# Taking the gated recurrence's logarithms in its projections, and loading its first pair of heads into tiles of the mixer that runs beside them

## The chip, the cores and the metric

One core of a Trainium2 chip runs the whole program. The metric is the device time of one execution in microseconds (us). A run's time is a little longer than the span of its profile, which lasts from the first to the last instruction. The engines are PE (matrix multiply; PEld is its weight load), DVE (vector), ACT (activation functions), POOL (GpSimd) and SP, whose queue issues most DMAs. Each engine works through its own instructions in the order in which they are written into the program.

## The reference, cut to what matters

Two transformer blocks over 512 tokens of width 1024. The second block also reads 256 context tokens and has three mixers side by side: a gated recurrence (4 heads, HGRN), a delta-rule recurrence (4 heads, RWKV) and a windowed attention (8 heads). Their outputs are concatenated, projected by `w_out`, and feed a mixture of 32 experts. The change touches the gated recurrence:

```python
def hgrn2_forget(f_pre, lb):
    f = lb + (1.0 - lb) * jax.nn.sigmoid(f_pre)
    log_f = jnp.log(jnp.maximum(f, HGRN_F_FLOOR))
    k = (1.0 - lb) * jax.nn.sigmoid(-f_pre)
    return to_heads(log_f, A_HEADS), to_heads(k, A_HEADS)
...
cum = jnp.cumsum(log_f, axis=3)                    # within a chunk
decay = exp(cum[t] - cum[s]) for s <= t
scores = jnp.einsum('bhntd,bhnsd,bhntsd->bhnts', q, k, decay)
o_intra = scores @ v;  q_in = q * exp(cum);  k_out = k * exp(cum[-1] - cum)
s = s * exp(cum[-1]) + k_out^T v                   # state from chunk to chunk
...
out = rms_norm(o_forward + flip(o_backward), gn_gain) * silu(g)
```

It runs forwards and backwards, over the context first and then over the latent tokens.

## The kernel before, in words

Block 1 runs first, up to about 800 us. Then comes block 2. `block2_in` makes its normalised input (`hchi`, `hclo` for 256 context tokens, `hlhi`, `hllo` for 512 latent ones, each as a high and a low part), and `rwkv_in` makes the inputs of the RWKV mixer by projections.

`rwkv` and `project` are traced one after the other, and the scheduler mixes them. `rwkv` handles six chunks of 128 tokens, each with a `front` (gates, decays, a 32x32 triangular solve that goes through DRAM by way of the tiles `rsc`, `rB`, `sX`) and a `back` (state update). `project` makes all other projections of the block, those of the attention and of the gated recurrence, by `gemm2` (one 128-column weight tile, split in a high and a low part by ACT at L299 and POOL at L300, then three matmuls for each of eight slices) or `tokens_of`. A result goes from PSUM by ACT into a staging tile `gst` (two buffers) and by an SP DMA to DRAM. Its order is: queries and keys of the attention (L1317), their row sums and reciprocal roots, the attention's values (L1300, L1308), the recurrence's values, queries, then for each pair of heads p and direction d the gate `f` and key `k` (two Sigmoids at L1360, scaled at L1361 and L1362, stored as `hfd` and `hkd`), and last the output gates (L1317 with Silu).

`hgrn` then loads all that for two pairs of heads (`hlf` by L1384, `hk` by L1389, `hq`, `hg`) into tiles on the right side of SBUF, where the tiles of `rwkv` were. It takes the logarithm of the gates: maximum (L1399), Ln with scale 8 (L1400), minus log 8 (L1401), and Ln of the latent keys into `hE` (L1406). The generator `pair` first handles the context (copy on POOL L1421, scan L1423, Exp L1432) and then seven levels (a hierarchical scheme that doubles the block length H from 1 to 64), each with Exps (L1470 to L1475), products, matmuls and four POOL additions (L1486 to L1489). The two pairs take turns. In between, pieces of the output projection run for the RWKV half (`out_first`: `mraw`, `wor`, `woh`, L1720), and after step 9 the first attention head. After the levels come the remaining heads, the rest of the output projection, the router, and the experts, whose weights (`er`) are loaded once the attention's tiles are free.

What sets the order: the Tile framework's scheduler places each engine's instructions by priority and by when it thinks inputs and buffers are there; a tile may reuse the bytes of an older one once all readers of that are done. `issue_after(logs.ins)` keeps the first Exps behind the last Ln on ACT.

Of the kernel before, what the change touches and what calls it, by code (L numbers as in the profile page):

```python
# [18 lines left out]
P = 128  # L19
# [139 lines left out]
def consts3():  # L159
    c = Pack()  # L160
    i = np.arange(P)
    c.add("ident", np.eye(P))
# [8 lines left out]
    f = np.arange(TC) % P  # L171
    c.add("hg_suf", np.broadcast_to((f != P - 1).astype(np.float32), (P, TC)))
    c.add("hg_pre", np.broadcast_to((f != 0).astype(np.float32), (P, TC)))
    return c


C2, C3 = consts2(), consts3()


# [60 lines left out]
def prep2(i):  # L240
# [4 lines left out]
    o["c2"], o["c3"] = C2.array(), C3.array()  # L245
# [27 lines left out]
class Kern:  # L273
# [601 lines left out]
    def c(self, name, rows=P):  # L875
        o, n = self.cat[name]
        return self.cst[:rows, o:o + n]
# [94 lines left out]
    def rwkv_in(self):  # L972
        nc, I, rw = self.nc, self.I, self.rw
        mu = self.v("mu")
# [18 lines left out]
        th, ad = (rw.tile([P, 768], F32, name=n) for n in ("rth", "rad"))  # L993
        k, v = (rw.tile([P, 2, 768], F32, name=n) for n in ("rk", "rv"))
# [25 lines left out]
    def rwkv(self):  # L1020
# [14 lines left out]
        kk = rw.tile([P, 2, 768], F32, name="rkk")  # L1035
# [241 lines left out]
    def project(self):  # L1277
# [4 lines left out]
        self.hqd, self.hgd = dram("hqd", 2, P, T), dram("hgd", 2, P, T)  # L1282
        self.hfd, self.hkd, self.hvd = dram("hfd", 2, 2, P, N), dram("hkd", 2, 2, P, N), dram("hvd", N, 256)
# [4 lines left out]
        def st(n):  # L1288
            return self.gs.tile([P, N], F32, tag="gst", name=self.name("gst"), bufs=2)[:, :n]
# [32 lines left out]

        sums = self.gp.tile([96, T], F32, tag="ss", name="nss", bufs=1)
# [16 lines left out]
        tokens(I["w_hi"], lambda i, o: rows(self.hvd, i, o))  # L1340


        l = self.v("lb")
        lb, nb = (self.gs.tile([P, 4], F32, name=n) for n in ("hlb", "hnb"))
        nc.vector.tensor_sub(lb, l, l)
        nc.scalar.activation(lb, lb, AF.Exp)
        nc.vector.reciprocal(nb, lb)
        nc.vector.tensor_mul(lb, lb, nb)
        nc.vector.tensor_sub(lb, lb, lb)
        nc.vector.tensor_scalar(nb, lb, -1.0, 1.0, OP.mult, OP.add)  # L1350
        for p in range(2):
            columns(I["w_hg"][p], self.hqd[p])
        for p in range(2):
            for d in range(2):
                c = 2 * d + p
                ps = self.gemm2(I["w_hg"][2 + c])
                f, k = st(N), st(N)
                for o, sign in ((f, 1.0), (k, -1.0)):
                    for x, t in zip((o[:, :TC], o[:, TC:]), ps):
                        nc.scalar.activation(x, t, AF.Sigmoid, scale=sign)  # L1360
                nc.vector.tensor_scalar(f, f, nb[:, c:c + 1], lb[:, c:c + 1], OP.mult, OP.add)  # L1361
                nc.vector.tensor_scalar(k, k, nb[:, c:c + 1], None, OP.mult)  # L1362
                nc.sync.dma_start(self.hfd[p, d], f)
                nc.sync.dma_start(self.hkd[p, d], k)
        for p in range(2):
            columns(I["w_hg"][8 + p], self.hgd[p], func=AF.Silu)

    def hgrn(self):
# [6 lines left out]
        def psum(n=T):  # L1375
# [3 lines left out]
        pairs = [([], [], hw.tile([P, T], F32, tag="hq", name=self.name("hq"), bufs=2),  # L1379
                  hw.tile([P, T], F32, tag="hg", name=self.name("hg"), bufs=2)) for _ in range(2)]  # L1380
        for p in range(2):
            for d in range(2):
                pairs[p][0].append(hw.tile([P, N], F32, tag="hlf", name=self.name("hlf"), bufs=4))
                nc.sync.dma_start(pairs[p][0][d], self.hfd[p, d])  # L1384
        self.h_loads = ()
        for p, (lf, kx, q, sgt) in enumerate(pairs):
            for d in range(2):
                kx.append(hw.tile([P, N], F32, tag="hk", name=self.name("hk"), bufs=4))
                nc.sync.dma_start(kx[d], self.hkd[p, d])  # L1389
            self.h_loads = self.h_loads[:1] + (nc.sync.dma_start(q, self.hqd[p]),)  # L1390
            if p == 0:
                others = self.out_first()
                next(others)
                vt = hw.tile([P, 6, 256], F32, name="hvt")
                nc.sync.dma_start(vt, self.hvd.rearrange("(i p) d -> p i d", p=P))
            self.h_loads = self.h_loads[:1] + (nc.sync.dma_start(sgt, self.hgd[p]),)
# [14 lines left out]
        def pair(p, lf, kx, q, sgt):  # L1411
# [4 lines left out]
            for d in range(2):  # L1416
# [14 lines left out]
                with self.tc.issue_after(logs.ins):  # L1431
                    nc.scalar.activation(e, e, AF.Exp)  # L1432
# [924 lines left out]
```

## Time and profile before

| | us |
|---|---|
| three runs | 2075.93, 2077.91, 2082.70 |
| median | 2077.91 |
| the profiled execution | 2081.68 |
| its span | 2079.9 |

| engine | busy us | share of the span |
|---|---|---|
| PE | 1839.3 | 88% |
| PEld | 1303.1 | 63% |
| DVE | 967.7 | 47% |
| ACT | 673.5 | 32% |
| POOL | 573.5 | 28% |

The mean clock granted to TensorE is 0.908 of full speed. A share is an average over very different stages; what the change touches lies between about 850 and 1435 us. In a timeline row the bracket gives how long the engine stood idle before the instruction and what ended that. SPq and ACTq rows are DMA issues.

### The profile page before, as it was taken

The numbers are of one execution on the slowest core, as the hardware profiler recorded it, in microseconds if no ns is written. First come the engines' busy times: TensorE is split into PE (matmuls) and PEld (weight loads), VectorE is DVE, ScalarE is ACT, GpSimd is POOL, SyncE is SP. The second block draws the span as 40 slices with busy tenths as digits, with TensorE's granted clock in tenths as the row PEclk, the third lists the DMA queues.
The fourth block names the chain that finished last, engine by engine and source line by source line (L and its number), as shares of the span: only waits on it lengthen the run. The fifth ranks groups of instructions, "written<-read, shape, count | busy, mean of one in ns | idle before, by whom it ended". The sixth has DMA issues, their size and how long they took to land. (4 is left out here: it accounts for less than half of the span.)

```text
span 2079.9 us, 30469 instructions
## 1 busy us (share of the span) xinstructions
PE 1839.3 (88%) x11941; PEld 1303.1 (63%) x11941; DVE 967.7 (47%) x2052; ACT 673.5 (32%) x1241; POOL 573.5 (28%) x405
## 2 busy tenths in 40 slices
PE   5978899898989999899998999558896999999996
PEld 3656566676757777776777877446675555544442
DVE  5443643575673116435755555576676322222110
ACT  6652324643443234442332223534332101000000
POOL 3222412444346555341211111472100110101011
PEclk9897899999989999996978789668998999999999
DMA  3111223355642225222312122733347999999997
GB/s 132 41 51 32 80 62 109 127 186 182 206 149 71 92 94 204 70 74 63 84 35 72 44 69 93 236 107 114 105 171 273 394 411 416 416 412 415 411 413 277
DMA packets 132668, 363.69 MB, mean 175 GB/s; under 512 B 43884, under 2 KB 63532, under 8 KB 107820
## 3 DMA queue, kind: packets, MB, share of 16 engines
q1 hardware_dynamic: 121916, 340.84, 44.3%
q10 hardware_dynamic: 5472, 15.05, 2.4%
q0 software_dynamic: 5136, 5.85, 1.4%
q8 instruction: 95, 1.56, 0.3%
q14 instruction: 49, 0.40, 0.1%
HBM read 333.02 MB, written 26.55 MB: 173 GB/s over the span
## 5 line engine op out<-in xcount | busy, mean ns | idle before, releaser
L300 POOL TENSOR_TENSOR lo<-wraw,hi 128x1024 fp32r<-128x1024 f32 (+1 forms) x127 | 298.5, 2351 | 587.9 <-ACT hi L299 518.4
L314 PE MATMUL g<-h1hi,hi 128*128 128x512 f32 (+1 forms) x584 | 251.8, 431 | 11.7 <-ACT gt L441 7.5
L316 PE MATMUL g<-h1hi,lo 128*128 128x512 f32 (+1 forms) x584 | 249.5, 427 | 6.5 <-POOL lo L300 6.5
L315 PE MATMUL g<-h1lo,hi 128*128 128x512 f32 (+1 forms) x584 | 251.2, 430 | 3.1 <-DVE h1lo L357 1.6
L2153 PE MATMUL gu<-er,xw 128*64 128x256 f32 x2048 | 237.1, 382 | 8.6 <-issue 3.0
L299 ACT ACTIVATE hi<-wraw 128x1024 fp32r<-128x1024 f32 (+1 forms) x127 | 127.5, 1004 | 313.8 <-PE g L315 154.5
L2153 PEld LDWEIGHTS gu<-er,xw 128*64 128x64 f32 x2048 | 145.3, 137 | 94.8 <-issue 19.9
L2182 POOL DMA_INDIRECT out_dram<-ey,sidx x32 | 49.5, 1547 | 403.6 <-DVE ey L2181 389.8
L314 PEld LDWEIGHTS g<-h1hi,hi 128*128 128x128 f32 (+1 forms) x584 | 117.5, 201 | 46.3 <-ACT gt L441 8.4
L316 PEld LDWEIGHTS g<-h1hi,lo 128*128 128x128 f32 (+1 forms) x584 | 116.9, 200 | 43.9 <-POOL lo L300 11.2
L315 PEld LDWEIGHTS g<-h1lo,hi 128*128 128x128 f32 (+1 forms) x584 | 117.1, 200 | 38.5 <-issue 8.8
L2178 PE MATMUL py<-er,es 128*64 128x512 f32 x512 | 120.4, 603 | 1.4 <-SPq L2224 1.0
L314 PE MATMUL g<-hlhi,hi 128*128 128x512 f32 x200 | 85.2, 426 | 5.0 <-ACT hlhi L951 4.6
L2156 ACT ACTIVATE eg<-gu 128x256 f32<-128x256 f32 x32 | 12.1, 383 | 226.5 <-PE gu L2153 226.5
L315 PE MATMUL g<-hllo,hi 128*128 128x512 f32 x200 | 85.4, 427 | 0.0
L316 PE MATMUL g<-hlhi,lo 128*128 128x512 f32 x200 | 85.3, 427 | 0.0
L2081 PE MATMUL tr<-h,S 128*128 128x512 f32 x256 | 75.1, 426 | 11.3 <-DVE xw L2090 6.7
L2181 DVE SCALAR_TENSOR_TENSOR ey<-py,wslot,g2row 128x512 f32<-128x512 f32 x32 | 24.0, 751 | 117.9 <-PE py L2178 117.9
L2178 PEld LDWEIGHTS py<-er,es 128*64 128x64 f32 x512 | 34.4, 137 | 61.4 <-issue 52.7
L2081 PEld LDWEIGHTS tr<-h,S 128*128 128x128 f32 x256 | 46.8, 198 | 37.4 <-issue 18.3
L898 DVE CUSTOM_DVE_ANT_0 aw<-aw,acc 128x1024 f32<-128x1024 f32 x48 | 64.8, 1355 | 7.7 <-DMA aw<-in_w_ada_dram 7.4
L2157 DVE TENSOR_TENSOR eh<-eg,gu 128x256 f32<-128x256 f32 x32 | 13.3, 417 | 116.5 <-ACT eg L2156 116.5
(659 smaller groups left out, 3689.3 us busy)
## 6 DMA issues: line engine op xcount, KB each, us to landing
er<-in_w_e_dram SPq DMA_DIRECT2D x192, 1024.0 KB
aw<-in_w_ada_dram SPq DMA_DIRECT2D x48, 512.0 KB
wraw<-in_w_qkv_dram SPq DMA_DIRECT2D x36, 512.0 KB
wraw<-in_w_g_dram SPq DMA_DIRECT2D x12, 512.0 KB
dxs<-draw SPq DMA_DIRECT2D x96, 64.0 KB
wraw<-in_w_rw_dram SPq DMA_DIRECT2D x9, 512.0 KB
wraw<-in_w_ga_dram SPq DMA_DIRECT2D x8, 512.0 KB
wraw<-in_w_gb_dram SPq DMA_DIRECT2D x8, 512.0 KB
```

Source lines behind the costliest of these rows:

```text
L299: nc.scalar.activation(hi, raw, AF.Copy)
L300: (lo_engine or nc.gpsimd).tensor_sub(lo, raw, hi.bitcast(F32))
L314: nc.tensor.matmul(ps, lh, rh, start=start, stop=False, **kw)
L315: nc.tensor.matmul(ps, lh, rl, start=False, stop=False, **kw)
L316: nc.tensor.matmul(ps, ll, rh, start=False, stop=stop, **kw)
L898: nc.vector.tensor_tensor_reduce(out=w, in0=w, in1=cc, scale=1.0, scalar=0.0, op0=OP.mult, op1=OP.add, accum_out=self.modl[:, m:m + 1])
L2081: nc.tensor.matmul(ps[:n], S[:, i, :n], self.h2[i][a][:, c], start=i + a == 0, stop=i + a == 4)
L2153: nc.tensor.matmul(ps[64 * c:64 * c + 64, a, :], xs(2 * i + k), w[:, k, a, c, :], start=i + k + a == 0, stop=i == 3 and k == 1 and a == 1, ...
L2157: nc.vector.tensor_mul(hid, g, ps[:, 1])
L2178: nc.tensor.matmul(py[64 * c:64 * c + 64], hs[:, k, 64 * i:64 * i + 64], part[:, k, c, :], start=i + k == 0, stop=i + k == 2)
L2181: nc.vector.scalar_tensor_tensor(y, py, w, self.g2, OP.mult, OP.mult)
L2182: nc.gpsimd.indirect_dma_start(out=self.O["out_0"].rearrange("t (h d) -> (t h) d", h=2), out_offset=bass.IndirectOffsetOnAxis(ap=idx, axis ...
```

## The change

The recurrence's gates, keys, queries, values and output gates are projected first, the attention's inputs last. The two logarithms are taken there: the gate's in place in its staging tile, the key's in a third one, stored in a new DRAM tile `hld`. The staging tag has three buffers. In `rwkv_in` the tiles `rth`, `rad`, `rk`, `rkk` move into a pool `rwf` of their own, which ends at the same address as before but lies below the other tiles. `hgrn` gets a pool `h0` on the left side, whose addresses (105856 to 124288) lie within those of `rwf` (106400 to 124832) but for the first 544, which no later tile before them uses; the first pair's gate, key, log key and query are loaded there. The second pair's stay in `hw`, and the output gates are loaded last. The identity and the scan mask move from the third pack of constants to a fourth, `c4`, which is loaded before `rwkv_in`. `issue_after` falls away.

```diff
@@ rwkv_in
+        th, ad = (self.rwf.tile([P, 768], F32, name=n) for n in ("rth", "rad"))
+        k, self.rw_kk = (self.rwf.tile([P, 2, 768], F32, name=n) for n in ("rk", "rkk"))
...
-        th, ad = (rw.tile([P, 768], F32, name=n) for n in ("rth", "rad"))
-        k, v = (rw.tile([P, 2, 768], F32, name=n) for n in ("rk", "rv"))
+        v = rw.tile([P, 2, 768], F32, name="rv")
@@ project
-            return self.gs.tile([P, N], F32, tag="gst", name=self.name("gst"), bufs=2)[:, :n]
+            return self.gs.tile([P, N], F32, tag="gst", name=self.name("gst"), bufs=3)[:, :n]
...
+        for p in range(2):
+            for d in range(2):
+                c = 2 * d + p
+                ps = self.gemm2(I["w_hg"][2 + c])
+                f, k = st(N), st(N)
+                for o, sign in ((f, 1.0), (k, -1.0)):
+                    for x, t in zip((o[:, :TC], o[:, TC:]), ps):
+                        nc.scalar.activation(x, t, AF.Sigmoid, scale=sign)
+                nc.vector.tensor_scalar(f, f, nb[:, c:c + 1], lb[:, c:c + 1], OP.mult, OP.add)
+                nc.vector.tensor_scalar(k, k, nb[:, c:c + 1], None, OP.mult)
+                nc.sync.dma_start(self.hkd[p, d], k)
+
+                nc.vector.tensor_scalar(f, f, 1e-20, None, OP.max)
+                nc.scalar.activation(f, f, AF.Ln, scale=8.0)
+                nc.vector.tensor_scalar(f, f, float(np.log(8.0)), None, OP.subtract)
+                nc.sync.dma_start(self.hfd[p, d], f)
+                l8 = st(T)
+                nc.scalar.activation(l8, k[:, TC:], AF.Ln, scale=8.0, bias=self.eps(1e-36))
+                nc.sync.dma_start(self.hld[p, d], l8)
+        for p in range(2):
+            columns(I["w_hg"][p], self.hqd[p])
+        tokens(I["w_hi"], lambda i, o: rows(self.hvd, i, o))
+        for p in range(2):
+            columns(I["w_hg"][8 + p], self.hgd[p], func=AF.Silu)
...
@@ hgrn
+        pairs, lk = [], []
+        gates = [self.hg.tile([P, T], F32, tag="hg", name=self.name("hg"), bufs=2) for _ in range(2)]
         for p in range(2):
...
+            to = hw if p else self.h0
+            lf, kx, le = ([to.tile([P, n], F32, tag=f"{t}{p}", name=self.name(t), bufs=2) for _ in range(2)]
+                          for t, n in (("hlf", N), ("hk", N), ("hE", T)))
+            pairs.append([lf, kx, (self.hg if p else to).tile([P, T], F32, tag=f"hq{p}", name=self.name("hq"), bufs=1)])
+            lk.append(le)
...
         for p, (lf, kx, q, sgt) in enumerate(pairs):
...
+            for src, dst in ((self.hfd, lf), (self.hkd, kx), (self.hld, lk[p])):
+                for d in range(2):
+                    nc.sync.dma_start(dst[d], src[p, d])
             self.h_loads = self.h_loads[:1] + (nc.sync.dma_start(q, self.hqd[p]),)
...
-        for lf, *_ in pairs:
-            for x in lf:
-                nc.vector.tensor_scalar(x, x, 1e-20, None, OP.max)
-                logs = nc.scalar.activation(x, x, AF.Ln, scale=8.0)
-                nc.vector.tensor_scalar(x, x, float(np.log(8.0)), None, OP.subtract)
-        lk = []
-        for _, kx, *_ in pairs:
-            lk.append([hw.tile([P, T], F32, tag="hE", name=self.name("hE"), bufs=4) for _ in range(2)])
-            for x, k in zip(lk[-1], kx):
-                logs = nc.scalar.activation(x, k[:, TC:], AF.Ln, scale=8.0, bias=self.eps(1e-36))
...
-                with self.tc.issue_after(logs.ins):
-                    nc.scalar.activation(e, e, AF.Exp)
+                nc.scalar.activation(e, e, AF.Exp)
@@ run
+                pool(es, "pc4", side="right")
+                self.c4 = self.pc4.tile([P, C4.n], F32, name="c4")
+                nc.gpsimd.dma_start(self.c4, self.I["c4"])
...
+                pool(right, "rwf", side="right")
...
+                        pool(e5, "hg")
+                        pool(e5, "h0")
```

How the scheduler's order moves, at three places. SP's queue at the solver of the mixer's fifth and sixth chunk (`rsc`, `rB`, `sX` and `AS` are the solver's tiles), before:

```order
L1145 DMA rsc_8128<-sX_8169 256x1x32 x4
L1125 DMA rsc_8538<-AS_8512 32x8x32 x2
L1148 DMA AS_8101<-rsc_8128 32x8x32 x4
L1127 DMA rB_8544<-rsc_8538 128x1x1024
L1318 DMA hqd<-gst_10072 128x512
L1318 DMA hqd<-gst_10106 128x512
L1363 DMA hfd<-gst_10165 128x768
L1364 DMA hkd<-gst_10166 128x768
```

and now, where `hlf`, `hk`, `hE` are the first pair's gate, key and log key:

```order
L1408 DMA hlf_10516<-hfd 128x768
L1408 DMA hlf_10517<-hfd 128x768
L1323 DMA nkc<-gst_10003 128x256
L1408 DMA hk_10518<-hkd 128x768
L1408 DMA hk_10519<-hkd 128x768
L1408 DMA hE_10520<-hld 128x512
L1408 DMA hE_10521<-hld 128x512
L1151 DMA rsc_8136<-sX_8177 256x1x32 x4
L1131 DMA rsc_8546<-AS_8520 32x8x32 x3
L1154 DMA AS_8109<-rsc_8136 32x8x32 x4
L1131 DMA rsc_8546<-AS_8520 32x8x32
L1325 DMA nqk<-gst_10003 128x512
```

The first pair's loads have come up from behind the mixer's end to stand ahead of the last but one solver's stores; the attention's stores stand where the recurrence's were. SP's queue at the mixer's end (`mix<-ry` stores its output), before:

```order
L1364 DMA hkd<-gst_10364 128x768
L1255 DMA mix<-ry 128x512
L1318 DMA hgd<-gst_10404 128x512
L1384 DMA hlf_10476<-hfd 128x768
L1384 DMA hlf_10478<-hfd 128x768
L1318 DMA hgd<-gst_10438 128x512
L1384 DMA hlf_10480<-hfd 128x768
L1384 DMA hlf_10482<-hfd 128x768
L1389 DMA hk_10484<-hkd 128x768
L1389 DMA hk_10486<-hkd 128x768
L1390 DMA hq_10472<-hqd 128x512
L1720 DMA mraw_10491<-mix 128x512
```

and now:

```order
L1261 DMA mix<-ry 128x512 x2
L1307 DMA nvd<-gst_10461 128x2x256
L1728 DMA mraw_10539<-mix 128x512
L1315 DMA nvw<-gst_10464 128x128 x4
L1728 DMA wor_10543<-in_w_o_dram 128x256
L1408 DMA hlf_10523<-hfd 128x768
L1315 DMA nvw<-gst_10470 128x128 x4
L1728 DMA mraw_10549<-mix 128x512
L1728 DMA wor_10553<-in_w_o_dram 128x256
L1408 DMA hlf_10524<-hfd 128x768
L1408 DMA hk_10525<-hkd 128x768
L1408 DMA hk_10526<-hkd 128x768
```

Behind the mixer's output no load of the first pair is left; those of the second pair (`hlf_10523` and on) stand behind the stores of the attention's window values. ACT in the second chunk's front (L1072 and L1078 are its Tanh, L1081 and L1087 its first Exp), before:

```order
L1072 ACTIVATE rt_6913<-rm_6926,rhb 128x128 x2
L299 ACTIVATE hi_9302<-wraw_9300 128x1024
L1081 ACTIVATE lam_6941<-rt_6937 128x8
L1091 ACTIVATE rt_6936<-rt_6936 128x512
L1082 ACTIVATE rt_6937<-rt_6937 128x512
L1317 ACTIVATE gst_9231<-g_9206 128x512
L307 DMA wraw_9400<-in_w_na_dram 128x1024
L1315 ACTIVATE gst_9292<-g_9242 128x256
L1328 ACTIVATE gst_9231<-gst_9231 128x512
L1132 ACTIVATE AHt_6959<-rm_6992 128x512
L1132 ACTIVATE AHt_6959<-rm_6998 128x512
L1142 ACTIVATE VS_7004<-rm_7007 64x8x64 x2
```

and now (L1345 the Sigmoid, L1351 and L1355 the two logarithms, L1138 and L1148 copies of the mixer):

```order
L1138 ACTIVATE AHt_6746<-rm_6785 128x512
L1351 ACT_TABLE_LOAD
L1351 ACTIVATE gst_9246<-gst_9246 128x768
L1148 ACTIVATE VS_6791<-rm_6794 64x8x64 x2
L1078 ACT_TABLE_LOAD
L1078 ACTIVATE rt_6920<-rm_6923,rhb 128x128 x2
L1078 ACTIVATE rt_6920<-rm_6924,rhb 128x128 x2
L1355 ACT_TABLE_LOAD
L1355 ACTIVATE gst_9259<-gst_9247,eps_9186 128x512
L1078 ACT_TABLE_LOAD
L1078 ACTIVATE rt_6921<-rm_6933,rhb 128x128 x2
L1078 ACTIVATE rt_6921<-rm_6934,rhb 128x128 x2
```

Where Copies and Squares of the attention stood between the mixer's instructions there are now Sigmoids and logarithms with table loads; in the whole program ACT has 88 table loads instead of 77.

## Rows read from the trace of the kernel before

**Rows 1.** the page, part 2: busy tenths and GB/s in 40 slices
```profile
PE   5978899898989999899998999558896999999996
...
PEclk9897899999989999996978789668998999999999
...
GB/s 132 41 51 32 80 62 109 127 186 182 206 149 71 92 94 204 70 74 63 84 35 72 44 69 93 236 107 114 105 171 273 394 411 416 416 412 415 411 413 277
```

**Rows 2.** busy time by stage; after POOL the clock, DMA share, GB/s
```profile
940.00:1300.00 360.00, 340.28 (x2956) 271.16 (x2955) 207.98 (x598) 103.41 (x185) 57.78 (x56) 0.83 0.22 65
1306.00:1333.00 27.00, 8.11 (x21) 5.14 (x20) 11.30 (x27) 12.42 (x20) 10.19 (x12) 0.58 0.89 287
1333.00:1405.00 72.00, 43.37 (x309) 34.69 (x307) 53.88 (x72) 31.46 (x77) 52.55 (x63) 0.71 0.41 133
1405.00:1537.00 132.00, 118.86 (x845) 84.98 (x846) 84.46 (x186) 56.44 (x115) 20.16 (x12) 0.88 0.28 86
1600.00:2060.00 460.00, 428.46 (x2895) 234.95 (x2890) 103.16 (x186) 42.80 (x94) 48.12 (x33) 1.00 1.01 411
```

**Rows 3.** timeline of SP's queue: start us, length, line, what, [idle before]
```profile
1304.04 0.32 SPq L1255 DMA_DIRECT2D mix<-ry  x1
...
1306.18 0.80 SPq L1384 DMA_DIRECT2D hlf<-hfd  x2
...
1308.71 0.94 SPq L1384 DMA_DIRECT2D hlf<-hfd  x2
```

**Rows 4.** timeline of ACT in the same stretch
```profile
1307.73 0.60 ACT L1317 ACTIVATE gst<-g 128x512 f32<-128x512 f32 x1 [4.18 <-PE g L316]
...
1310.13 1.28 ACT L1400 ACT_TABLE_LOAD   x1 [1.80 <-DVE hlf L1399]
...
1311.42 1.58 ACT L1400 ACTIVATE hlf<-hlf 128x768 f32<-128x768 f32 x2
...
1326.69 0.72 ACT L1406 ACTIVATE hE<-hk,eps 128x512 f32<-128x512 f32 x1 [4.83 <-DMA hk<-hkd]
...
1330.36 1.28 ACT L1432 ACT_TABLE_LOAD   x1
...
1331.65 1.33 ACT L1432 ACTIVATE ht<-ht 128x256 f32<-128x256 f32 x4
...
1332.89 0.43 ACT L1470 ACTIVATE ht<-hlf 128x256 f32<-128x256 f32 x1
```

**Rows 5.** timeline of DVE in the same stretch
```profile
1309.50 0.56 DVE L1399 TENSOR_SCALAR hlf<-hlf 128x768 f32<-128x768 f32 x1 [3.15 <-DMA hlf<-hfd]
...
1315.75 0.56 DVE L1399 TENSOR_SCALAR hlf<-hlf 128x768 f32<-128x768 f32 x1 [2.21 <-DMA hlf<-hfd]
...
1316.69 0.68 DVE L1423 TENSOR_TENSOR_SCAN ht<-ht,c 128x256 f32<-128x256 f32 x1
```

**Rows 6.** timeline of POOL in the same stretch
```profile
1313.61 0.39 POOL L1421 COPY ht<-hlf 128x256 f32<-128x256 f32 x1 [4.76 <-DMA hlf<-hfd]
...
1316.84 0.73 POOL L1427 COPY ht<-hlf 128x256 f32<-128x256 f32 x1 [2.83 <-DVE hlf L1401]
```

**Rows 7.** groups of ACT, 940 to 1308: count, busy, mean ns, idle
```profile
L1360 ACT ACTIVATE gst<-g 128x256 f32<-128x256 f32 (+1 forms) x16 | 7.4, 487 | 18.7 <-DMA hfd<-gst 14.8 <-PE g L316 2.7 <-DMA hkd<-gst 1.1
...
L363 ACT ACT_TABLE_LOAD x4 | 5.1, 1283 | 0.1
```

**Rows 8.** timeline of SP's queue, stores of the window values
```profile
1140.92 5.18 SPq L1308 DMA_DIRECT2D nvw<-gst  x8
```

**Rows 9.** tile rkk: its last reader, with first and last start
```profile
L1098 DVE SCALAR_TENSOR_TENSOR rt<-rt,rkk x12: 409/414/2603, 935.2 to 1197.4; 128x256 f32<-128x256 f32 x12
```

**Rows 10.** timeline of SP's queue, stores of the solver's result
```profile
1210.16 2.52 SPq L1145 DMA_DIRECT2D rsc<-sX  x4
```

**Rows 11.** waits of ACT in the seven levels: total us, times, longest
```profile
ACT woh L299 <- DMA wor<-in_w_o_dram: 22.6, 3, 11.9
```

**Rows 12.** timeline of SP's queue, first weights of the experts
```profile
1537.43 17.67 SPq L2120 DMA_DIRECT2D er<-in_w_e_dram  x14
```

More of the change, by code (lines that the diff above doesn't have):

```diff
@@ L170, in consts3, with consts4 @@
     c.add("rt_half", np.broadcast_to((i[:, None] >= 64), (P, 48)).astype(np.float32))
-    f = np.arange(TC) % P
-    c.add("hg_suf", np.broadcast_to((f != P - 1).astype(np.float32), (P, TC)))
-    c.add("hg_pre", np.broadcast_to((f != 0).astype(np.float32), (P, TC)))
-    return c
-C2, C3 = consts2(), consts3()
+    return c
+def consts4():
+    c = Pack()
+    c.add("ident", np.eye(P))
+    c.add("hg", np.broadcast_to((np.arange(TC + 1) % P != 0).astype(np.float32), (P, TC + 1)))
+    return c
+C2, C3, C4 = consts2(), consts3(), consts4()
 def hgrn_masks():
@@ L875, in c @@
     def c(self, name, rows=P):
-        o, n = self.cat[name]
-        return self.cst[:rows, o:o + n]
+        tile, at = (self.c4, C4.at) if self.c4 is not None and name in C4.at else (self.cst, self.cat)
+        o, n = at[name]
+        return tile[:rows, o:o + n]
     def v(self, name, rows=P):
@@ L1033, in psum @@
             return self.rmp.tile([P, T], F32, tag="rm", name=self.name("rm"))[:, :n]
-        kk = rw.tile([P, 2, 768], F32, name="rkk")
+        kk = self.rw_kk
         for p in range(2):
@@ L1319, in columns @@
             return o
+        l = self.v("lb")
+        lb, nb = (self.gs.tile([P, 4], F32, name=n) for n in ("hlb", "hnb"))
+        nc.vector.tensor_sub(lb, l, l)
+        nc.scalar.activation(lb, lb, AF.Exp)
+        nc.vector.reciprocal(nb, lb)
+        nc.vector.tensor_mul(lb, lb, nb)
+        nc.vector.tensor_sub(lb, lb, lb)
+        nc.vector.tensor_scalar(nb, lb, -1.0, 1.0, OP.mult, OP.add)
+        for p in range(2):
[21 more added lines that the diff above has]
+            columns(I["w_hg"][8 + p], self.hgd[p], func=AF.Silu)
         sums = self.gp.tile([96, T], F32, tag="ss", name="nss", bufs=1)
@@ L1339, in project @@
             tokens(I["w_nv"][2 * hf:2 * hf + 2], lambda i, o: window_rows(hf, i, o))
[L1340 to L1366, printed above, removed]
     def hgrn(self):
@@ L1394, in hgrn @@
                 vt = hw.tile([P, 6, 256], F32, name="hvt")
[L1395 to L1406 removed]
+        nc.sync.dma_start(vt, self.hvd.rearrange("(i p) d -> p i d", p=P))
+        for p in range(2):
+            nc.sync.dma_start(pairs[p][3], self.hgd[p])
         outs = []
@@ L1468, in pair @@
                 E, K = tmp(), tmp()
-                with self.tc.issue_after(logs.ins):
-                    nc.scalar.activation(hv(E)[:, :, 0, :], hv(SB)[:, :, 0, :], AF.Exp)
-                    nc.scalar.activation(hv(E)[:, :, 1, :], hv(PF)[:, :, 1, :], AF.Exp)
+                nc.scalar.activation(hv(E)[:, :, 0, :], hv(SB)[:, :, 0, :], AF.Exp)
+                nc.scalar.activation(hv(E)[:, :, 1, :], hv(PF)[:, :, 1, :], AF.Exp)
                 nc.vector.tensor_mul(E, E, q)
```

20 lines of the change are left out of this document (7 added, 13 removed).

## The prediction

> **What bounds the kernel now.** I read the page first, then the stages, then the seam between the two recurrences engine by engine. The last quarter is set by the experts' weights: from 1600 to 2060 us the DMA engines are busy the whole time at 411 GB/s [rows 1, 2], and the first of these loads goes out at 1537.43 us [rows 12], when the attention's tiles are free. Nothing in that stage is touched. What the stages ahead of it save therefore moves the whole stream forward, and what they lose delays it. From 940 to 1300 us, where the RWKV mixer and the projections run side by side, PE is busy 340.28 of 360 us while ACT has 103.41 of work [rows 2]. Then comes a hole: from 1306 to 1333 us PE works 8.11 of 27 us at a granted clock of 0.58, with the DMA share at 0.89 [rows 2]. In the levels after it (1333 to 1405) POOL, with 52.55 of 72 us, and DVE, with 53.88, are the fullest.
>
> The hole is a chain. The mixer's last store is issued at 1304.04, the first gate load at 1306.18 [rows 3] and is used at 1309.50 [rows 5]; maximum, table load, Ln and subtraction follow, for the second pair again from 1315.75 [rows 4, 5], then the logs of the keys, of which one waits 4.83 us for its load at 1326.69, then a table load at 1330.36, four Exps, and at 1332.89 the first Exp of the first level [rows 4]. From the mixer's last store to the first level that is 28.85 us.
>
> **The change part by part.**
>
> *The seam.* The logs, their two table loads and the first pair's loads leave this chain. What is late next is the second pair: ACT's order has the context Exps of both pairs ahead of the first level, and the second pair's second gate stands on SP behind four stores of the attention's window values. I rebuild the chain with the mixer's end left at 1304.04. Its store has landed at 1306.18, as before. The load of the mixer's output for the output projection takes what the first gate load took, 3.32 us (1306.18 to 1309.50): 1309.5. Its cast comes ahead of the projections' last copy on ACT; both at the price of that copy, 0.60 [rows 4]: 1310.7. Four window stores at 5.18/8 = 0.65 us [rows 8]: 1313.3. Two more issues at 0.40 (0.80 for two) [rows 3]: 1314.1. The gate load lands after 3.32 us or, like the third one before (1308.71 to 1315.75) [rows 3, 5], after 7.04: 1317.4 to 1321.1. POOL's copy (0.39 to 0.73) [rows 6], the scan (0.68) [rows 5] and one Exp (1.33/4) [rows 4] add 1.4 to 1.7. So the first level starts between 1318.8 and 1322.8, middle 1320.8, instead of 1332.89: 10.1 to 14.1 us less. I take 12.1. The early loading of the first pair by itself is worth nothing in this sum, since the second pair ends the wait; it keeps 2.4 MB out of the crowded stretch, which speaks for the lower end.
>
> *ACT in the projections.* Eleven more table loads at 1283 ns [rows 7] are 14.1 us; four Ln of 0.79 (1.58 for two) and four of 0.72 [rows 4] are 6.0. That is 20.1 us more on ACT early in the mixer, where Copies stood. ACT is idle for 257 of 360 us there, so what counts is how often the mixer, and PE behind it, waits for an ACT that is busy with a log. PE is idle for 19.7 of 360 us, 5.5%; I charge the same share of the 20.1 us, 1.1. All of it on the path would be 20.1. On the other side, the two-buffer staging made ACT's Sigmoids wait 14.8 us for stores [rows 7]; a third buffer could take some away, but the log keeps a staging tile longer, so I count no gain; the bound is 14.8. DVE's eight scalings move along with about 0.56 each [rows 5], 4.5 us beside 152 idle ones: nothing.
>
> A rule weighed here. The rows show a table load of 1283 ns [rows 7], and behind the one at 1310.13 the Ln starts at 1311.42, with no gap beyond the load's own 1.28 us [rows 4]. The Trainium skill (ScalarE: Activation LUTs, "What ACT_TABLE_LOAD costs") charges a drain of about 1380 ns on top, about 2.66 us for each switch, and its "Rules for kernel authors" say to do all of one table set before switching: a rule against this change, which puts logarithms between Tanhs. By it eleven switches would be an estimated 29 us of ACT instead of 14.1. The trace shows no such drain, so the sum goes by 1.28.
>
> *The first pair's loads, early.* They stand on SP ahead of the solver's stores for the fifth chunk. The last reader of their place (`rkk`) starts at 1197.4 and takes 0.41 us [rows 9]; the solver's stores go out at 1210.16 [rows 10]. Four loads of 0.39 MB and three of 0.26 are 2.36 MB, at 287 GB/s [rows 2] 8.2 us: from 1197.8 to 1206, ahead of the stores by 4. Cost nothing; if they come late, up to 8.2 us on a chain that runs through DRAM. The 1.05 MB of new stores of the log keys fall where 65 GB/s move [rows 2]: nothing.
>
> *The rest.* The same matmuls are done in another order; at the mixer's end the share of projection work still outstanding is nearly the same, so PE's end near 1307 stays. The levels, the attention and the router keep their order and shift as a whole.
>
> Sum: -12.1 + 1.1 = -11.0 us. Against the profiled execution, 2081.68, that is 2070.7; it was 3.8 us above the median of 2077.91, so against the median it is 2066.9, and I say 2067. This case's own range, with 10.1 to 14.1 of gain and up to 6 us for ACT's part, is 2063 to 2074.
>
> **The rivals.**
>
> *More than the seam.* In the levels ACT waits 22.6 us in three pieces for weights of the output projection [rows 11], which stand on SP among the attention's loads. The second of the four now stands ahead of the second head's window loads. Half of the wait gone would be 11.3 us more: 2056; all of it 2044. Against it: each of these weights waits for the one buffer of the weight before, which the change leaves as it is.
>
> *The queue gives it back.* The first pair's loads, or the attention's stores behind which the second pair now stands, hold SP. If the solver's stores wait out the 8.2 us, the mixer ends that much later: 2075, no change that can be told. For it: SP is one queue in order, and the order puts seven loads that wait for buffers ahead of them. Against it: the 4 us of air, and PE with projection work to fill.
>
> *Slower: logs on the mixer's chain.* The mixer is a chain of fronts and backs whose Tanh and Exp share ACT's queue with the Sigmoids and logs. If all 20.1 us fall between its steps in the first three chunks, and PE, whose order is fixed, waits with it, the mixer ends 19 us later than I count, and the kernel takes 2067 + 19 = 2086. It decides the sign from the point where more than 12.1 of the 20.1 us land on the chain. For it: PE is nearly full from 940 on, so lost PE time is not made up later. Against it: ACT is idle 71% of that stage.
>
> **How the numbers follow.** Forecast 0.58, more than the seam 0.17, the queue 0.15, slower 0.10. A difference under 0.3% (6.2 us, from 2071.7 to 2084.1) can't be told from none. Faster by more: 0.52 of the forecast, all 0.17 of the second, 0.05 of the third, 0.74. Within: 0.06 + 0.10 + 0.02 of the last = 0.18. Slower: 0.08. The range of 8 in 10 leaves out the outer part of the second case and the last one: 2050 to 2079.
>
> **What would show it.** Right: no Ln with a 128x768 tile after the mixer's store, the first level's Exp 14 to 19 us behind that store instead of 28.85, PE's hole shorter by 10 to 14, the first weights of the experts near 1526, and the stream after that unchanged at about 411 GB/s. ACT's step would be wrong if PE's idle time from 940 to the mixer's end grew by more than 6 us or the last mixer store came later than 1308; the queue's if the solver's stores of the fifth chunk waited for SP; the seam's if the first level came later than 23 us behind the mixer, above all if its last wait ends on a load of the second pair. The whole is wrong if the levels, 72 us long now, change their own length by more than the seam does.

## The result: slower by 1.0%, and the profile after

Eight runs of each kernel: 2106.21 us (2094.55 to 2109.14) after, 2081.64 (2065.82 to 2093.06) before, ratio 1.0104 with a 95% interval of 1.0081 to 1.0128. The prediction was 2067, faster; of the 39.2 us between, 3.7 are its base, since the three runs that it went by have a median of 2077.91. The profiled execution of the new kernel took 2106.58 us, its span is 2104.8 at a mean granted clock of 0.898 (before: 2081.68, 2079.9, 0.908).

The page, part 2, of the kernel after:
```profile
PE   5988898989899999898899989648896999999996
...
PEclk9877799899979999997768889768898999999999
...
GB/s 131 41 50 37 75 61 112 141 177 188 205 125 70 92 109 196 70 68 101 86 43 70 56 113 42 203 111 103 107 137 277 380 412 416 417 413 415 411 413 277
```
Against [rows 1] the experts' stream is the same: of the last ten slices the eight between the first and the last read 380 to 417 GB/s here and 394 to 416 there.

I cut the time ahead of it at five rows that both kernels have: the store of `r1d`, the mixer's last store (`mix<-ry`), the first Exp of the first level, HGRN's first store (`mix<-ho`), and the first experts' weights (`er`). SP's queue of the kernel after (start us, length, line, what):
```profile
847.40 0.34 SPq L936 DMA_DIRECT2D r1d<-r  x1
...
1325.36 0.32 SPq L1261 DMA_DIRECT2D mix<-ry  x1
...
1453.17 0.31 SPq L1560 DMA_DIRECT2D mix<-ho  x1
...
1560.89 4.06 SPq L2128 DMA_DIRECT2D er<-in_w_e_dram  x8
```
and ACT around the first level:
```profile
1329.11 0.42 ACT L1441 ACTIVATE ht<-ht 128x256 f32<-128x256 f32 x1 [2.02 <-DVE hdec L1434]
1329.87 0.42 ACT L1441 ACTIVATE ht<-ht 128x256 f32<-128x256 f32 x1 [0.35 <-DVE hdec L1440]
...
1336.78 0.42 ACT L1441 ACTIVATE ht<-ht 128x256 f32<-128x256 f32 x1 [4.05 <-DVE hdec L1434]
...
1341.95 0.42 ACT L1441 ACTIVATE ht<-ht 128x256 f32<-128x256 f32 x1 [3.16 <-DVE hdec L1440]
1342.28 0.42 ACT L1478 ACTIVATE ht<-hlf 128x256 f32<-128x256 f32 x1
```
Of the kernel before, the rows that [rows 3, 4, 12] don't have:
```profile
841.28 0.34 SPq L931 DMA_DIRECT2D r1d<-r  x1
...
1434.18 7.75 SPq L1552 DMA_DIRECT2D mix<-ho  x2
```

| from, to | before | after | difference |
|---|---|---|---|
| start to r1d's store (code untouched) | 841.3 | 847.4 | +6.1 |
| to the mixer's last store | 462.8 | 478.0 | +15.2 |
| to the first level (the seam) | 28.9 | 16.9 | -12.0 |
| to HGRN's store (the levels) | 101.3 | 110.9 | +9.6 |
| to the experts' first weights | 103.2 | 107.7 | +4.5 |

The first row is spread between single executions, of instructions that the change doesn't touch: in the fourteen profiles below, this store stands between 839.0 and 844.4 (in e4, whose code up to there is that of the kernel after, at 842.4). The seam did what was forecast, 12.0 us against 12.1. No Ln with a 128x768 tile is left behind the mixer's store, and what the first level waits for last is the second pair: its two context Exps at 1336.78 and 1341.95. But the mixer took 15 us longer and the levels took 9.6 us of the seam back.

**The mixer.** One window from 100 us behind r1d's store to the mixer's last store; after the span come the busy times of PE, PEld, DVE, ACT and POOL, the granted clock, the DMA share and GB/s. Before:
```profile
941.28:1304.08 362.80, 344.02 (x2972) 274.52 (x2973) 208.89 (x600) 106.53 (x188) 57.37 (x55) 0.84 0.22 65
```
After:
```profile
947.40:1325.40 378.00, 348.16 (x2936) 275.97 (x2936) 211.86 (x606) 119.75 (x198) 59.74 (x58) 0.81 0.24 72
```
PE's idle time is 362.80 - 344.02 = 18.8 us before and 378.00 - 348.16 = 29.8 after, and the granted clock fell from 0.84 to 0.81. The two granted levels are 1.2 and 2.4 GHz, so a mean of 0.84 over 362.8 us is 116 us at the lower one, 0.81 over 378.0 is 144. The views give the clock with two digits; summed over stretches of 10 us it is 119 and 142 us, and half of the difference, 11.5 us, is what the lower clock would cost if PE worked all through it. The two accounts overlap, since idle time at the lower clock counts in both: the rows show more idle time and a lower clock, and don't divide the 15.2 us between them. What PE did before it fell, in one place, 160 to 190 us behind r1d's store, before:
```profile
1001.28:1011.28 10.00, 10.00 (x80) 6.44 (x78) 7.49 (x27) 2.44 (x4) 3.50 (x8) 1.00 0.39 107
1011.28:1021.28 10.00, 9.78 (x140) 7.07 (x139) 5.96 (x24) 3.87 (x10) 0.11 (x1) 1.00 0.27 67
1021.28:1031.28 10.00, 8.70 (x85) 6.83 (x85) 9.83 (x18) 5.50 (x11) 4.04 (x8) 1.00 0.31 89
```
and after, with the PE row that ends the gap:
```profile
1007.40:1017.40 10.00, 5.21 (x53) 3.78 (x52) 9.38 (x22) 2.60 (x4) 5.12 (x3) 0.88 0.70 232
1017.40:1027.40 10.00, 9.77 (x113) 9.02 (x113) 5.58 (x22) 0.74 (x2) 0.00 (x0) 0.50 0.01 2
1027.40:1037.40 10.00, 10.00 (x81) 7.98 (x82) 5.13 (x19) 4.08 (x11) 0.00 (x0) 0.60 0.00 0
```
```profile
1017.63 1.05 PE L652 MATMUL pw<-rXT,AS 32*32 32x32 f32 x16 [5.01 <-DVE rXT L1166]
```
PE stood 4.8 of 10 us, waiting for a copy on DVE (`rXT`) behind the solver's rows, and then ran 20 us at 0.50 and 0.60. Before, projection matmuls stood there. Over the whole window PE's waits for `rXT` are 4.4 us in one piece before and 7.7 in two after; those for `AH`, another step of the mixer on DVE, grew from 4.8 to 9.4.

**The levels.** ACT's waits for the output projection's weights, which were 22.6 us [rows 11], of the kernel after:
```profile
ACT woh L303 <- DMA wor<-in_w_o_dram: 37.7, 4, 16.3
```
The last three of these loads, on SP, and the ACT rows that wait for the first and the last of them:
```profile
1384.54 0.38 SPq L1728 DMA_DIRECT2D wor<-in_w_o_dram  x1
...
1394.46 0.32 SPq L1728 DMA_DIRECT2D wor<-in_w_o_dram  x1
...
1405.05 0.33 SPq L1728 DMA_DIRECT2D wor<-in_w_o_dram  x1
```
```profile
1393.21 0.42 ACT L303 ACTIVATE woh<-wor 128x256 fp32r<-128x256 f32 x1 [16.33 <-DMA wor<-in_w_o_dram]
...
1417.07 0.42 ACT L303 ACTIVATE woh<-wor 128x256 fp32r<-128x256 f32 x1 [12.45 <-DMA wor<-in_w_o_dram]
```
The last such cast of the kernel before:
```profile
1396.87 0.42 ACT L299 ACTIVATE woh<-wor 128x256 fp32r<-128x256 f32 x1 [9.59 <-DMA wor<-in_w_o_dram]
```
The loads stand among the attention's loads, each waits for the one buffer of the weight before, and the next level's Exps are queued behind. From the mixer's last store to the last of these casts it is 1396.87 - 1304.04 = 92.8 us before and 1417.07 - 1325.36 = 91.7 after. So I take it that the levels' end hangs on this chain, which starts at the mixer's end and didn't move, and that a first level that is 12 us earlier only waits longer inside; e4 to e8 below test it.

### The profile page after: what moved, and what is told of

The parts are those of the page before. It is cut to its first block, busy times and chain, and to the rows that moved or that the text cites. A ratio compares the mean times of both kernels' runs of the same rounds, so it can differ in the third digit from the quotient of the medians.

```text
span 2104.8 us, 30489 instructions
## 1 busy us (share of the span) xinstructions
PE 1857.1 (88%) x11941; PEld 1315.1 (62%) x11941; DVE 963.2 (46%) x2052; ACT 687.4 (33%) x1252; POOL 571.6 (27%) x406
## 5 line engine op out<-in xcount | busy, mean ns | idle before, releaser
L320 PEld LDWEIGHTS g<-h1hi,lo 128*128 128x128 f32 (+1 forms) x584 | 118.1, 202 | 45.4 <-POOL lo L304 11.9
```

The lines of the kernel that those rows point to most:

```text
L320: nc.tensor.matmul(ps, ll, rh, start=False, stop=stop, **kw)
```

## Experiments

All times are medians; ratios are to the kernel before, run beside it. The stages (mixer, seam, levels) are cut at the rows above, in the profiled execution of each kernel.

| run | time, us | ratio (95%) | mixer | seam | levels |
|---|---|---|---|---|---|
| before | 2081.64 | 1 | 462.8 | 28.9 | 101.3 |
| after | 2106.21 | 1.0104 (1.0081 to 1.0128) | 478.0 | 16.9 | 110.9 |
| e1 order only | 2103.66 | 1.0101 (1.006 to 1.0142) | 476.4 | 29.9 | 101.1 |
| e2 order, logs | 2117.93 | 1.0171 (1.0132 to 1.0211) | 486.4 | 21.8 | 123.1 |
| e3 after, attention first | 2083.51 | 1.0005 (0.9975 to 1.0035) | 455.7 | 13.4 | 116.6 |
| e4 after, two buffers | 2091.59 | 1.0035 (1.0005 to 1.0066) | 487.2 | 14.3 | 102.1 |
| e5 before, two buffers | 2072.1 | 0.9945 (0.9921 to 0.997) | 463.9 | 29.5 | 89.9 |
| e6 = e1, two buffers | 2093.43 | 1.0048 (1.0024 to 1.0071) | 487.1 | 29.4 | 90.3 |
| e7 = e2, two buffers | 2098.27 | 1.0069 (1.0042 to 1.0097) | 483.3 | 22.3 | 102.8 |
| e8 = e3, two buffers | 2069.64 | 0.9928 (0.9899 to 0.9957) | 468.1 | 15.1 | 99.8 |
| e9 = e8, nx on SP | 2070.5 | 0.9954 (0.9923 to 0.9986) | 466.6 | 15.9 | 95.0 |
| e10 gates first | 2090.06 | 1.0053 (1.0027 to 1.0078) | 482.6 | 31.5 | 89.1 |
| e11 gates last | 2076.98 | 0.9982 (0.9956 to 1.0008) | 462.8 | 35.3 | 90.8 |
| e12 = e4, more logs | 2100.38 | 1.008 (1.0051 to 1.011) | 492.1 | 11.9 | 106.2 |
| e13 gates second | 2086.48 | 1.0012 (0.9991 to 1.0032) | 470.7 | 31.5 | 88.8 |
| e14 after, gates second | 2074.24 | 0.9964 (0.9937 to 0.999) | 468.5 | 15.2 | 105.8 |

The kernel after and e4 have the same mixer instructions, and their profiles show 478.0 and 487.2: a single profile places the mixer within some 9 us. So what a part costs is read from the ratios, and the stages only say where. The time of the kernel before differed from one group of runs to the next (2079.6 to 2084.6), so steps between groups go by the ratios too; a step of under some 0.4% is at the edge of what these intervals can tell.

**e1, e2, e3: which part.** e1 is the kernel before with HGRN's block of the projections moved, and nothing else:

```
+        l = self.v("lb")
...
+            columns(I["w_hg"][8 + p], self.hgd[p], func=AF.Silu)
         sums = self.gp.tile([96, T], F32, tag="ss", name="nss", bufs=1)
```

e2 adds the logs, with the stores, loads and third staging buffer that go with them:

```
+                nc.scalar.activation(f, f, AF.Ln, scale=8.0)
+                nc.scalar.activation(l8, k[:, TC:], AF.Ln, scale=8.0, bias=self.eps(1e-36))
...
-                logs = nc.scalar.activation(x, x, AF.Ln, scale=8.0)
```

e3 is the kernel after with the attention's block moved back:

```
+        sums = self.gp.tile([96, T], F32, tag="ss", name="nss", bufs=1)
...
+            tokens(I["w_nv"][2 * hf:2 * hf + 2], lambda i, o: window_rows(hf, i, o))
         l = self.v("lb")
```

Expected of e1: 

> The kernel before with one edit: HGRN's projections come ahead of the attention's; the logs stay behind the mixer, no early loads, two staging buffers. In the two traces so far the time from the store of r1d to the mixer's last store is 462.8 us before (1304.04 - 841.28) and 478 us after. Theory A (the logs, 20 us of ACT, land on the mixer's chain): the order alone leaves 463 within 4 us, and the time within 0.3% of the kernel before. Theory B (the order itself: other matmuls stand between the mixer's steps, with PE idle and a lower granted clock as the result): 473 to 478 us here already, and the time 8 to 15 us above before, since nothing of the seam is gained. Theory C (the first pair's early loads hold SP and POOL): as theory A here.

Expected of e2: 

> The kernel of e1 with the logarithms taken in the projections as in the kernel after, three staging buffers, and the log keys stored and loaded; all loads of both pairs still stand behind the mixer. Theory A (logs on the chain): the stretch from r1d's store to the mixer's last store grows by 10 to 15 us over that of e1, to about 475, and the time is about 2090 to 2100. Theory B (order): no more than 3 us over e1. Theory C (early loads): 463 to 466 us, and the time 5 us or more below the kernel before, since the logs have left the seam.

Expected of e3: 

> The kernel after with the attention's projections put back ahead of HGRN's (logs in the projections, the first pair in tiles of its own, three staging buffers stay). Theory A (logs on the chain): the logs now stand beside the mixer's last chunks; the mixer's last store is still 8 us or more late. Theory B (order): the stretch from r1d's store to the mixer's last store returns to 463 to 466 us, and the time to 2075 to 2088. Theory C (early loads): they can't be early any more, as their data come last, so 463 to 466 too; e2 tells it from B.

The order alone costs 1.0%, 20 to 21 us (more than the 8 to 15 that I gave it), and with the old order the rest of the change costs nothing: theory B. e2 is 14 us above e1, more than B allowed; its trace has that in the levels (123.1, where ACT's longest wait for a weight is 22.8 us) and in the mixer, 10 us longer than e1's as theory A had it. From e2 to the kernel after, the early loads and what goes with them give it back. By the ratios: +1.01% order, +0.70 logs, -0.67 early loads, together the 1.04 of the change. The window as above, of e1 and of e6, its repeat with two weight buffers:
```profile
943.26:1319.64 376.38, 348.94 (x2965) 275.81 (x2965) 203.18 (x598) 107.35 (x186) 58.74 (x56) 0.83 0.22 62
```
```profile
942.63:1329.73 387.10, 356.56 (x2965) 280.15 (x2965) 203.15 (x598) 107.34 (x186) 58.69 (x56) 0.81 0.21 61
```
PE is idle 27.4 and 30.5 us, 9 to 11 more than in the kernel before and in e5 (19.4): that part of the order's price is in every profile with the gates first (27 to 31 us; 49 in e12, which adds logs). The clock differs between these two executions of one order as well, so its part is read from all executions: the mean granted clock is 0.910 over e5's twelve and 0.904 over e6's, which (twice what the clock lacks to 1, times the span) is 373 and 400 us at the lower level. Half of the difference, 14 us, stands beside 22 us between the two mean times. So both belong to the price of the order, idle PE and a lower clock; how much of the lower clock is only what the idle time brings, these runs don't show.

**e4 to e8: the weights' buffer.** One character in each:

```
-                           for n, d, b in (("r", F32, 1), ("h", F32R, 2), ("l", F32R, 2)))
+                           for n, d, b in (("r", F32, 2), ("h", F32R, 2), ("l", F32R, 2)))
```

Expected of e4: 

> The kernel after with a second buffer for the output projection's weight pieces in the levels. Theory W (the levels end with the chain of these eight loads, which stand on SP among the attention's loads and of which each waits for the one buffer; ACT waits 37.7 us for them against 22.6 before, and from the mixer's last store to the last of them it is 91.7 us in both kernels, so the seam's 12 us come back there): ACT's wait for them falls below 20 us, the levels (first Exp of the first level to HGRN's store, 110.9 us) shrink by 8 to 15, and the time falls by that, to about 2092 to 2099. Rival (SP itself is late with everything, the buffer doesn't matter): the waits keep 30 us or more and the time stays within 0.3% of the kernel after, 2100 to 2112.

Expected of e5: 

> The kernel before with the second buffer for the output projection's weight pieces, nothing else. Theory W (the eight weight loads set the end of the levels in the kernel before as well, where ACT waits 22.6 us for them): from the mixer's last store to HGRN's store 130.1 us now, 118 to 124 then, and the time 6 to 12 us below the kernel before. Rival (before the change POOL and DVE set the levels, and the loads became the limit only when the seam grew short): the stretch stays at 128 to 131 us and the time within 0.3% of the kernel before.

Expected of e6: 

> The kernel of e1 (before with HGRN's projections first) with the second weight buffer. If the order's price lies in the mixer alone, this is 15 to 22 us slower than e5, as e1 is 20 us slower than before, with r1d's store to the mixer's last store again 10 us or more above 463. If part of e1's price came through the weight loads, the distance to e5 falls below 12 us.

Expected of e7: 

> The kernel of e2 (order and logs, late loads) with the second weight buffer. e2 is 14 us slower than e1, of which its trace puts +10 in the mixer, -8 in the seam and +22 in the levels with ACT's waits for the weights. If the levels' part is the weight chain, it goes: HGRN's store 116 to 124 us behind the mixer's store, and the time 3 us below to 6 us above e6. If the logs as such cost 10 us in the mixer in every run, it stays 2 to 6 above e6; if that was the spread between single executions, it falls 3 to 8 below e6, since the logs have left the seam.

Expected of e8: 

> The kernel of e3 (the change without its new order) with the second weight buffer. e3's trace gains 15.5 us in the seam and 7 in the mixer against before and gives 15.3 back in the levels, with 36.1 us of ACT's waits for the weights. Theory W: the levels fall from 116.6 to about 102 us, and the time to 2066 to 2074, faster than both kernels. Rival (SP late with all loads): 2080 to 2086.

Theory W held in all five, by the times; of the stretches that it forecast, e7's from the mixer's last store to HGRN's store, 125.1 us, came just above its 116 to 124. ACT's waits for these loads, of e2 and of e7:
```profile
ACT woh L299 <- DMA wor<-in_w_o_dram: 36.9, 4, 22.8
```
```profile
ACT woh L299 <- DMA wor<-in_w_o_dram: 3.3, 1, 3.3
```
In the other four they are 0.3 us or nothing, and the time falls by 10 to 20 us, in the kernel before by 0.55%: this chain bounded the levels before the change too, and that could have been read from [rows 11]. The steps in this setting, in per cent of the kernel before: order +1.03 (e6 over e5, 21 us), logs +0.21 (e7 over e6, 4 us), early loads and what goes with them -0.34 (e4 under e7, 7 us); the last two have intervals that meet. The seam shows both gains: 29.4 with the order alone, 22.3 with the logs gone, 14.3 with the first pair loaded early. Still, the levels are 10 to 13 us longer wherever the seam is short (89.9 and 90.3 against 99.8 to 102.8): from the mixer's last store to HGRN's store it is 119.3 us in e5 and 116.4 and 114.9 in e4 and e8, so of 14 to 15 us in the seam 3 to 4 are left, and e8 is no faster than e5 beyond their intervals. ACT in e8:
```profile
1363.11 0.49 ACT L1483 ACTIVATE ht<-hE,eps 128x256 f32<-128x256 f32 x1
1374.99 0.31 ACTq L1590 DMA_DIRECT2D nx<-nqk  x1
1375.42 0.42 ACT L1478 ACTIVATE ht<-hlf 128x256 f32<-128x256 f32 x1 [11.82 <-PE g L319]
...
1382.94 0.31 ACTq L1590 DMA_DIRECT2D nx<-nqk  x1
1383.37 0.42 ACT L303 ACTIVATE woh<-wor 128x256 fp32r<-128x256 f32 x1 [6.12 <-DMA nvw<-nvw]
```
Two loads of the attention's next heads (`nx`) are issued from ACT's own queue; ACT reaches them before they may go and stands 11.8 and 6.1 us with the levels' Exps behind.

**e9: those loads on SP**, in e8:

```
-                nc.scalar.dma_start(swapped[r:r + 32], ...
+                nc.sync.dma_start(swapped[r:r + 32], ...
```

Expected: 

> The kernel of e8 with the attention's swapped query and key loads (nx) issued on SP's queue instead of ACT's. In e8's trace ACT stands 11.8 and 6.1 us in the levels, each just ahead of such an issue (1374.99 and 1382.94), with the Exps of the next level queued behind. Theory V (after the weights the next limit is this issue on ACT's in-order queue; it comes up because the levels start 14 us earlier and the attention doesn't): ACT's two waits go, the levels fall from 99.8 to 88 to 94 us, and the time to 2058 to 2066. Rival (POOL's additions set the levels, or SP then holds the weight loads as long): 2068 to 2074, no gain.

ACT's two waits are gone and the levels fell to 95.0, but the time didn't (2070.5): the rival has it. In their place ACT waits for PE before it casts weights into `woh`:
```profile
ACT woh L303 <- PE g L319: 15.7, 4, 9.9
```
From HGRN's store to the experts' weights the profile shows 117.9 us where e8 has 102.8, in an execution 11 us above its median, so where the rest of the gain went isn't settled.

**e10, e11, e13, e14: which half of the order.** The same blocks in other orders, all with two weight buffers. G is the four gate projections, Q HGRN's queries, values and output gates, K the attention's queries and keys, V its values; e5 is K V Q G with the output gates last, e6 is G Q K V.

```
e10   G K V Q        e11   Q K V G        e13, e14   K G Q V
```

Expected of e10: 

> The kernel of e5 (before, two weight buffers) with only the four gate projections ahead of the attention's; HGRN's queries, values and output gates stay last. e6, where all of HGRN's come first, is 21 us slower than e5. Theory X (the price is the queries and values beside the mixer's second chunk, where PE stood idle for 7.4 of 20 us in e1): this stays within 6 us of e5, 2066 to 2078, with the mixer at 460 to 468 us. Theory Y (the gates are the wrong filler for the first chunk, or the attention's values are for the last one): 2084 to 2096, the mixer at 474 us or more.

Expected of e11: 

> The kernel of e5 with HGRN's queries, values and output gates ahead of the attention's projections, the four gates last as before: the other half of e6's order. Theory X (queries and values are the poor filler): 2080 to 2096, the mixer 8 us or more above 464, with idle on PE where they stand. Theory Y (the gates): within 6 us of e5, 2066 to 2078. If each half costs about half of e6's 21 us, what counts is how much of the attention's work is pushed into the last two chunks.

Expected of e13: 

> The kernel of e5 with HGRN's projections between the attention's queries and keys (first) and its values (last). e10, gates first, is 18 us slower than e5; e11, gates last, 5 us. If the price is the gates beside the mixer's first chunks, they now stand from its third chunk on: within 6 us of e5, 2066 to 2078. If what counts is that the attention's values come last, beside the mixer's end: 2084 to 2096.

Expected of e14: 

> The kernel of e4 (after with two weight buffers: logs, early loads) with the order of e13. If the gates beside the first chunks are the price, the mixer comes back to 460 to 470 us while the first pair can still be loaded before the mixer ends: the seam at 12 to 17 us, the time 2064 to 2076, at or below e8's 2070. If the values at the end are the price, 2084 to 2094 as e4.

Gates first costs 1.08% against e5 (22 us by the ratios, 18 by the medians), gates last 0.37%, with intervals that meet: theory Y, against what I had read from one gap. The same window as above, of e5 and of e10:
```profile
942.73:1306.63 363.90, 344.47 (x2976) 275.09 (x2976) 208.91 (x600) 106.28 (x187) 57.54 (x55) 0.84 0.22 64
```
```profile
943.10:1325.70 382.60, 355.46 (x2965) 280.11 (x2965) 204.73 (x598) 108.72 (x187) 59.70 (x57) 0.81 0.21 62
```
PE is idle 19.4 and 27.1 us, the clock 0.84 and 0.81: by stretches of 10 us 120 and 143 us at the lower level, worth 11.6 of the 18.7 us between the two spans. e13 and e14 fall into different branches of what I expected. With K first and G second the kernel before is still 0.67% above e5 (its mixer 7 us), at the time that I gave if the values at the end are the price; moving K ahead of the gates gave back only 0.36 of the 1.03%. The kernel after gains 0.71 of the 1.07% between e4 and e8 and lands in the branch of the gates. So gates at the very head cost about 1% (e6, e10), and the rest differs between the two kernels. How many gaps an order leaves on PE, and why, I can't work out from the order; that stays open.

**e12: more ACT.** In e4, on each of the eight gate tiles:

```
+                    nc.scalar.activation(o, o, AF.Ln, scale=8.0)
+                    nc.scalar.activation(o, o, AF.Exp, scale=1.0, bias=self.eps(-float(np.log(8.0))))
```

Expected: 

> The kernel of e4 (after with two weight buffers) with a log and an Exp that undo each other on each of the eight gate tiles before they are used: 16 more activations at 0.79 us, 15 more table loads at 1.283 us, together 32 us more of ACT in the early mixer, and 8 more maxima at 0.56 us on DVE. Theory B (ACT has room, the change's 20 us of logs cost the mixer nothing that can be told, the order does): within 6 us of e4's 2091.6. Theory A (logs land on the mixer's chain at the rate at which they are added): at half of the 32 us, 2107; at all, 2124.

The mixer's window of e4 and of e12:
```profile
942.41:1329.61 387.20, 355.93 (x2936) 283.68 (x2936) 210.90 (x606) 119.59 (x198) 59.27 (x58) 0.79 0.22 70
```
```profile
942.71:1334.80 392.09, 342.88 (x2840) 268.61 (x2841) 208.71 (x610) 151.03 (x230) 60.74 (x59) 0.79 0.23 70
```
8.8 us over e4, from 31.4 us more ACT (119.6 to 151.0) and eight more maxima on DVE: 0.28 for each us of ACT, more than theory B said and far from A. The intervals of the two ratios meet, so the 8.8 us is known to some 7 us either way and the rate to 0.1 to 0.5. By it the change's 20.1 us are an estimated 5.6 us, beside the 4 us between e7 and e6. Its rows also settle the rule weighed in the prediction; e12's ACT:
```profile
988.20 1.28 ACT L1348 ACT_TABLE_LOAD   x1
989.50 0.94 ACT L1348 ACTIVATE gst<-gst,eps 128x768 f32<-128x768 f32 x1
...
991.41 1.28 ACT L1358 ACT_TABLE_LOAD   x1
992.70 0.72 ACT L1358 ACTIVATE gst<-gst,eps 128x512 f32<-128x512 f32 x1
```
The activation starts 1.29 us behind the start of the load, with no gap between. The drain that the Trainium skill (ScalarE: Activation LUTs, "What ACT_TABLE_LOAD costs") adds is not seen here. That page's advice to finish one table set before switching ("Rules for kernel authors") was not tested by itself: e12 adds the switches together with the activations, and the two together cost time.

## Why the prediction was wrong, step by step

*The bound* was right: the stream at 410 GB/s is unchanged, and `er` came 23.5 us later and the span 24.9.

*The rest* is the step that failed: "The same matmuls are done in another order; at the mixer's end the share of projection work still outstanding is nearly the same, so PE's end near 1307 stays." The amount of work was right, but its cost isn't a constant. Other matmuls stood between the mixer's steps, PE was idle 11 us more in gaps of up to 5 us, and ran some 23 us more at the lower clock. e1 and e6 show that the order does this, e6 and e10 that the gates at the head are enough; why those matmuls leave more gaps stays open. I had the rows for it: the mean clock of 0.83 in that stage [rows 2] says that a third of it ran at the lower level, and I used these rows only for busy time. None of my rivals was this one; the slower rival put the loss on ACT. e1 shows 20 to 21 us for the order alone, nearly twice the whole gain that I forecast.

*The levels* "shift as a whole" failed too. ACT's waits for the weights stood in [rows 11] as a possible further gain; they were the chain that sets the end of the levels, so the seam's 12.0 us ended in longer waits (22.6 to 37.7 us). Another wait took the place of the one removed, one stage further than I looked. With the buffer most of the seam's gain still goes, to the attention's loads on ACT's queue (e8), and with these on SP in part to waits for PE (e9).

*The seam* was right in place and size: 12.0 against 12.1, the last wait the second pair's; to 0.1 us that is luck, as the forecast had 4 us between its ends, and e3 and e4 show a seam of 13.4 and 14.3 where the kernel after shows 16.9. That the early loads are worth nothing was wrong: without them and what goes with them the seam is 22.3 instead of 14.3, and the time 7 to 14 us higher.

*ACT in the projections*: the sign was right, the size off: 1.1 us against some 4 to 6. PE's idle share, 0.055, was too small a rate; the measured one is 0.28, roughly.

*The queue* was right: SP issued the first pair's loads at 1216.94 to 1220.32, and the solver's stores behind them at 1224.05, so SP stood free for 3.7 us in between, where I had 4.
```profile
1216.94 0.80 SPq L1408 DMA_DIRECT2D hlf<-hfd  x2
...
1219.24 1.08 SPq L1408 DMA_DIRECT2D hE<-hld  x2
1224.05 2.52 SPq L1151 DMA_DIRECT2D rsc<-sX  x4
```

The check that I had set caught it: the mixer's last store was to come no later than 1308, and came at 1325.36, and PE's idle time was to grow by no more than 6, and grew by 11. But it was written for ACT's step, and would have blamed the wrong part; only e1 told them apart.

## What to carry to other kernels

Moving equal work to another place beside a latency chain is not free: run the new order by itself first, as e1 did, and price PE time at the granted clock of the stage, not only at its busy share. A stall that goes at the head of a stage is worth what the chain that ends the stage gains, so follow that chain (here eight small weight loads with one buffer, on a shared queue) before booking the gain. The second buffer alone, 1 KB per partition, gave 0.55%, about what the whole change was meant to; with the old order and the rest of the change (e8) it is the fastest that I measured, 0.72% under the kernel before, though not told apart from e5.

## What the runs showed of the hardware

One instruction order ran at different granted clocks from one execution to the next: the kernel after and e4 have the same mixer instructions, with 29.8 and 31.3 us of idle PE, but 142 and 166 us of the window at the lower level (by stretches of 10 us); e3 and e8, alike in the same way, have 20.8 and 23.2 us idle, but 99 and 123 at the lower level. Half of each difference, 12 us, is as large as what their windows differ by, 9.2 and 12.4. So one profile can't tell what an order costs by way of the clock, while its idle time comes back within some 3 us (27.4 and 30.5 in e1 and e6, 18.8 and 19.4 in the kernel before and e5).

On DVE, two of the solver's rows in the gap above (kernel after) took ten times as long as their neighbours. Each ran beside POOL's split of a weight and ended within 0.1 us of it:
```profile
1008.20 2.42 DVE L631 TENSOR_TENSOR sX<-sX,stmp 128x69 f32<-128x69 f32 x1
...
1011.95 0.22 DVE L631 TENSOR_TENSOR sX<-sX,stmp 128x60 f32<-128x60 f32 x1
1012.21 2.31 DVE L630 TENSOR_TENSOR stmp<-sX,rB 128x76 f32<-128x76 f32 x1
```
```profile
1008.10 2.42 POOL L304 TENSOR_TENSOR lo<-wraw,hi 128x1024 fp32r<-128x1024 f32 x1 [3.08 <-issue]
...
1012.08 2.35 POOL L304 TENSOR_TENSOR lo<-wraw,hi 128x1024 fp32r<-128x1024 f32 x1 [1.55 <-ACT hi L303]
```
At the 0.23 us of their neighbours the two would have ended 4.3 us sooner, so an estimated 4.3 of PE's 5.01 us gap are theirs. All solver rows of over 1 us stand beside such a split, 9 of 372 in the kernel before, 11 after and 7 in e1: they are no more frequent where the order alone was changed, so they don't explain its price.
